# Three quarters of an MLP's first product as seven products of blocks, with tokens halved

## The chip, the cores and the metric

The kernel runs on one core of one Trainium2 chip. The metric is the device time of one execution in microseconds. One run is profiled as well; its rows and its trace are read below. PE is TensorE's matmul row, PEld its weight loads, DVE is VectorE, ACT is ScalarE, POOL is GpSimd and SP issues most of the transfers.

## The reference

A two-layer encoder with 512 tokens of 1024 features, batch 1, all in float32. Layer 0 mixes with stick-breaking attention, layer 1 with a gated linear recurrence; each is followed by the MLP, which is what changes here.

```
for layer in range(2):
    h = rms_norm(x, norm_mix[layer])
    x = x + (stick_breaking_attention(h, ...) if layer == 0 else rglru_block(h, ...))
    h = rms_norm(x, norm_mlp[layer])
    u = relu(h @ mlp_w1[layer])            # 512 x 1024 @ 1024 x 4096
    x = x + (u * u) @ mlp_w2[layer]        # 512 x 4096 @ 4096 x 1024
return rms_norm(x, norm_final)
```

## The kernel before

Activations lie with features on the 128 partitions and tokens along the free dimension: `x[c]` is a chunk of 128 features by 512 tokens, c = 0..7. A float32 product is made of three float32r matmuls: each operand is split into a high half (a cast, on ACT) and a low half (operand minus high half, on DVE), and high x high, low x high and high x low are summed in a bank. For the MLP's input the halves are `xgh` and `xgl`. For a slab of weights `raw`, 128 x 1024, they are `wh` and `wl`; the DVE instruction that makes `wl` is called a cut below. Four pairs of buffers `wh`/`wl` exist.

The MLP goes through the 4096 hidden features in four quarters of 1024 (`Mlp.quarters`).

*First product* (`squared`): for each of eight chunks of 128 hidden features, a slab of `w_m1` is loaded, cut, and multiplied with all tokens: 8 steps of k by 3 matmuls of 512 columns, so 192 matmuls a quarter (lines 209 to 211). ACT applies relu and square into `u`.

*Second product* (`down`): tokens, hidden features and outputs are halved, and the 2 x 2 blocks are multiplied by the seven products P1 to P7 (a scheme of Winograd's kind). `u` holds per unit of 256 hidden features the four blocks, from which DVE makes four sums in place (`sums`); `split` makes their high halves (`bh`, `sh`) on ACT and their low halves (`bl`, `sl`) on DVE. Blocks of weights `b11`, `b12`, `b22`, 128 x 2 x 512, are loaded ahead (`load`), `b21` on use. P5, P6, P7 and P4 need sums of blocks, made in place on DVE (line 865); only in the last quarter P7's and P4's (layer 0) or P4's (layer 1) are made by an accumulating transfer from POOL's queue. Each product is made for two halves g of the quarter ("P5 1" is P5 for the second half): 2 token slices x 2 x 3 matmuls of 512 columns, 12 a product, 168 a quarter (line 877). `collect` adds a finished bank, scaled per token, into `c`.

The order of PE is as written; the other engines' queues are put in order by the compiler's scheduler and are then fixed. Two dense chunks of the next quarter's first product are put ahead of each second product but the last:

```
                for c in range(2):
                    self.squared(q4 + 1, c)
                self.down(q4)
                self.sums(0)
                self.split(0)
```

In layer 1 the residual `x` is transposed and added to the output in the last quarter (`between`); in layer 0 the output is transposed back and added to `x` after it (`feature`). `x` stays in SBUF meanwhile.

Of the kernel before, what the change touches and what calls it, by code (L numbers as in the profile page):

```python
# [48 lines left out]
def hybrid_encoder(  # L49
# [10 lines left out]
    w_m1: bass.AP,  # L60
    w_dn: bass.AP,
# [666 lines left out]
    class Mlp:  # L728
# [10 lines left out]

        PRODUCTS = {  # L740
            "P1": (0, "b11", None, "X", 0, False),
            "P5": (4, "b11", "b12", "V", 3, False),
            "P6": (5, "b11", "b22", "X", 1, True),
            "P3": (6, "b22", None, "V", 1, False),
            "P7": (1, "b12", "b22", "X", 3, True),
            "P2": (2, "b21", None, "W", 0, False),
            "P4": (3, "b11", "b21", "X", 2, False),
# [5 lines left out]
        def __init__(self, ctx, layer):  # L753
            self.layer, self.sq, self.first = layer, Squares(), None
            self.mp = ctx.enter_context(tc.tile_pool(name=f"mlp{layer}", bufs=2))
            self.c = [
                self.mp.tile([P, 2, S], F32, tag=f"c{i}", name=f"c{i}", bufs=1) for i in range(4)
            ]
            self.begun, self.a = set(), {}
            self.turns = count()  # L760
            self.blocks = ExitStack()
            self.bp = self.blocks.enter_context(tc.tile_pool(name=f"blocks{layer}", bufs=2))
            self.u, self.raws = {}, {}
# [9 lines left out]
        def squared(self, q4, c, ready=None):  # L773

            if self.first is None:
                self.first = [self.bank() for _ in range(2)]
                ws = [slab(w_m1[self.layer, i]) for i in range(2)]
                beside(ws, xgh, xgl, self.first, {})
            if self.first:
                ps = self.first.pop(0)  # L780
            else:
                ps = dense(
                    w_m1[self.layer, q4 * C + c], xgh, xgl, halves=ready, ps=self.bank()
                )
            j, a = divmod(c, 2)
            if a == 0:
                self.u[j] = self.mp.tile([P, BLOCKS, HS], F32, tag="u", name="u", bufs=1)
            t = self.u[j][:, 2 * a : 2 * a + 2, :].rearrange("p i n -> p (i n)")
            A.activation(t, ps, AF.Relu)
            A.activation(t, t, AF.Square)  # L790
            if q4 == 0:

                if c in range(2, C - 2):
                    for i in range(2):
                        self.sq.chunk(2 * (c - 2) + i, x[2 * (c - 2) + i])
                if c == C - 1:
                    self.rr = self.sq.inv_squares(self.bank())
            return t

        def sums(self, j):  # L800

            u = self.u[j]
            for out, x, y, op in (
                (4, 1, 3, ALU.subtract), (5, 4, 0, ALU.subtract), (6, 5, 2, ALU.add),
                (1, 0, 1, ALU.subtract),
            ):
                V.tensor_tensor(u[:, out, :], u[:, x, :], u[:, y, :], op)  # L807

        def split(self, j):
            if j < 2:  # L810
                n = BLOCKS * HS
                h, l = (
                    t.rearrange("p c s -> p (c s)")[:, j * n : (j + 1) * n].rearrange(
                        "p (i n) -> p i n", n=HS
                    )
                    for t in (bh, bl)
                )
            else:
                h, l = (
                    self.bp.tile([P, BLOCKS, HS], F32R, tag=t, name=t) for t in ("sh", "sl")  # L820
                )
            u = self.u[j]
            A.copy(h, u)  # L823
            self.ready = V.tensor_tensor(l, u, f(h), ALU.subtract)  # L824
            self.a[j] = h, l

        def weights(self, q4, g, tag):
            return w_dn[self.layer, q4, g, *self.SOURCES[tag]]

        def load(self, q4):  # L830

            for g in range(2):
                for tag in ("b11", "b12", "b22"):
                    t = self.bp.tile([P, 2, S], F32, tag=tag, name=tag)
                    nc.sync.dma_start(out=t, in_=self.weights(q4, g, tag))
                    self.raws[tag, g] = t
# [10 lines left out]
        def block(self, q4, name, g, far):  # L847

            _, b, to, *_ = self.PRODUCTS[name]
            if b == "b21":  # L850
                t = wpool.tile([P, C, P], F32, tag="raw", name="raw", bufs=3)
                t = t.rearrange("p (j k) f -> p j (k f)", j=2)
                nc.sync.dma_start(out=t, in_=self.weights(q4, g, b))
                self.raws[b, g] = t
            raw = self.raws[b, g]
            if name in far:

                G.dma_start(out=raw, in_=self.weights(q4, g, to), accum_op=ALU.add)  # L858
            elif to:

                ahead = None
                if far and (name, g) != ("P5", 0):
                    ahead = self.ready if name == "P5" else self.before
                with tc.issue_after(ahead.ins) if ahead else nullcontext():
                    self.sum = V.tensor_tensor(raw, raw, self.raws[to, g], ALU.add)  # L865
            return self.operand(raw)

        def times(self, name, g, i, w, ps, new, cols=slice(0, S)):
# [4 lines left out]
            for jj in range(2):  # L873
                h, l = self.a[2 * g + jj]
                first, last = new and g == jj == 0, g == jj == 1
                for n, (x, y) in enumerate(((h, wh), (h, wl), (l, wh))):
                    PE.matmul(  # L877
                        ps, x[:, block, ts], y[:, jj, cols], start=first and n == 0,
                        stop=last and n == 2, skip_group_check=not new,
                    )  # L880
# [12 lines left out]
        def down(self, q4, far=(), end=None):  # L893
            sums, last_cut = {}, {}

            def product(name, g, w=None):
                w = w or self.block(q4, name, g, far)
# [13 lines left out]
            if end is None:  # L911
                for name in ("P1", "P5", "P6", "P3", "P7", "P2", "P4"):
                    for g in range(2):
                        product(name, g)
                return

            order = [("P1", 0), ("P5", 0), ("P2", 0), ("P1", 1), ("P2", 1), ("P5", 1)]
            order += [(name, g) for name in ("P6", "P3", "P7", "P4") for g in range(2)]
            ws = {}

            def prepare(*at):

                if at != ("P7", 1):
                    self.before = self.cut
                ws[at] = self.block(q4, *at, far)
                last_cut[at[0]] = self.cut
# [8 lines left out]

        def quarters(self, between, far, end):
            loaded = {}
            for q4 in range(NQ):
                last = q4 == NQ - 1
                for c in range(2 * (q4 > 0), C):  # L940

                    with tc.high_priority() if last and c > C - 3 else nullcontext():
                        self.squared(q4, c, loaded.pop(c, None))
                        if c % 2:
                            self.sums(c // 2)
                            self.split(c // 2)
                    if last and c == C - 3:
                        loaded = {i: slab(w_m1[self.layer, q4 * C + i]) for i in (C - 2, C - 1)}
                    if c == 3 - 3 * (q4 == 0):
                        self.load(q4)  # L950
                    between(q4, c)
                if last:
                    self.down(q4, far, end)
                    break

                for c in range(2):
                    self.squared(q4 + 1, c)
                self.down(q4)
                self.sums(0)
                self.split(0)  # L960
            self.blocks.close()

    with ExitStack() as mctx:
        mlp = Mlp(mctx, 0)
        squares = Squares()
# [23 lines left out]
        def between(q4, c):  # L989
            if (q4, c) == (0, C - 1):  # L990
                soft.send(mlp.ready)

        mlp.quarters(between, ("P7", "P4"), end)
# [186 lines left out]
    with ExitStack() as mctx:  # L1180
# [3 lines left out]
        def between(q4, c):  # L1184

            t = c - 2
            if q4 < NQ - 1 or t not in range(NB):
                return
            for h in range(2):
# [5 lines left out]
                V.tensor_tensor(mlp.y(t, h), mlp.y(t, h), pt, ALU.add)  # L1195

        gb = lp.tile([P, D], F32, tag="gb", name="gb")
        nc.sync.dma_start(out=gb, in_=g_final.broadcast_to([P, D]))
# [16 lines left out]
        def scaled(t, h, cols=slice(0, S)):  # L1215
            y = mlp.y(t, h)[:, cols]
            G.tensor_tensor(y, y, gb[:, h * S : (h + 1) * S][:, cols], ALU.mult)

        def finish(t, h, i, cut=None, last=None):
# [8 lines left out]
            with tc.issue_after(last.ins) if last else nullcontext():  # L1228
                V.scalar_tensor_tensor(
                    y[:, cut:], y[:, cut:], rt, gb[:, h * S : (h + 1) * S][:, cut:],  # L1230
# [31 lines left out]

        mlp.quarters(between, ("P4",), end)
# [65 lines left out]
```

## Time and profile before

| | us |
|---|---|
| median of 3 runs | 1076.51 |
| lowest and highest | 1075.07, 1077.06 |
| the profiled execution | 1076.9 |
| its span | 1075.1 |

In the span PE is busy 1059.4 us, DVE 782.4, ACT 599.6 and POOL 166.8. Layer 0's MLP lies at about 250 to 583 us of the span, layer 1's from about 734 on. A row of grouped instructions reads: line, engine, operation, tiles, shapes, count, busy time and mean ns of one, idle time ahead of them and who ended it. A row of the timeline reads: start in us, duration, engine, line, tiles, and in brackets the idle time before it.

### The profile page before, as it was taken

Reading aid. Unit: us, or ns where it says so; the run is one execution under the profiler, and the core shown is the slowest. Engines: PE = TensorE matmul, PEld = TensorE weight load, DVE = VectorE, ACT = ScalarE, POOL = GpSimd, SP = SyncE. Lnnn points to the kernel's source line nnn. Section 1 sums busy time; section 2 is a strip of 40 time slices with the busy share of each in tenths; the row PEclk is TensorE's granted clock in tenths of the full one; section 3 lists DMA queues with packets and bytes.
Section 4 is the critical chain, followed back from the end, with each engine's and each line's share of the span. In section 5 each row is a group of like instructions: output and inputs, shape, how many; then the busy total and the mean of one; then the engine's idle time right before and its main releaser. Section 6 shows DMA issues by size and latency. Waiting matters only on the chain.

```text
span 1075.1 us, 13570 instructions
## 1 busy us (share of the span) xinstructions
PE 1059.4 (99%) x5004; PEld 879.4 (82%) x5004; DVE 782.4 (73%) x1020; ACT 599.6 (56%) x888; POOL 166.8 (16%) x192
## 2 busy tenths in 40 slices
PE   9999999999999999999999999999999999999997
PEld 7888888888888888888878777888888888888875
DVE  7788787838686596597578878974676597497667
ACT  6777676826554543544546477944554544544346
POOL 2344443510000000000001655000000000000005
PEclk9999999999999999999999999999999999999999
DMA  7745454517215206206341785252215206305104
GB/s 236 198 117 148 122 147 108 170 52 249 85 49 187 79 31 187 96 20 191 84 98 60 180 211 129 87 191 82 79 43 190 82 22 189 103 20 176 59 6 112
DMA packets 44033, 125.70 MB, mean 117 GB/s; under 512 B 7744, under 2 KB 8512, under 8 KB 43968
## 3 DMA queue, kind: packets, MB, share of 16 engines
q1 hardware_dynamic: 41088, 115.94, 34.8%
q0 software_dynamic: 2304, 8.39, 4.5%
q8 instruction: 39, 0.64, 0.2%
q10 hardware_dynamic: 576, 0.52, 0.1%
q14 instruction: 26, 0.21, 0.1%
HBM read 104.91 MB, written 2.10 MB: 100 GB/s over the span
## 4 chain that ended last, share of the span: by engine, by line
PE 86%; DVE 5%; ACT 3%; issue 2%; POOL 2%; DMA 1%; SPq 0%; ACTq 0%; DVEq 0%; POOLq 0%
PE ps_t L877 8%; PE ps_acc L877 7%; PE ps_o L877 6%; PE ps_acc L211 6%; PE ps_acc L209 6%; PE ps_acc L210 6%; PE ps_z L877 5%; PE ps_t L209 4%; PE ps_t L210 4%; PE ps_t L211 4%; PE ps_o L209 4%; PE ps_o L211 4%; PE ps_o L210 4%; PE ps_z L210 3%; PE ps_z L211 3%; PE ps_z L209 3%
## 5 line engine op out<-in xcount | busy, mean ns | idle before, releaser
L204 DVE TENSOR_TENSOR wl<-raw,wh 128x1024 fp32r<-128x1024 f32 (+2 forms) x126 | 130.5, 1052 | 89.7 <-ACT wh L197 89.5
L843 ACT CAST wh<-b 128x1024 fp32r<-128x1024 f32 x96 | 100.0, 1048 | 122.2 <-PE ps_t L877 23.3
L197 ACT CAST wh<-raw 128x1024 fp32r<-128x1024 f32 (+2 forms) x136 | 119.5, 898 | 66.9 <-PE ps_acc L877 10.2
L844 DVE TENSOR_TENSOR wl<-b,wh 128x1024 fp32r<-128x1024 f32 x96 | 116.5, 1221 | 41.6 <-ACT wh L843 40.9
L209 PE MATMUL ps_acc<-xgh,wh 128*128 128x512 f32 x288 | 116.0, 403 | 1.0 <-ACT wh L178 0.9
L210 PE MATMUL ps_acc<-xgh,wl 128*128 128x512 f32 x288 | 112.7, 391 | 0.3 <-DVE wl L179 0.3
L211 PE MATMUL ps_acc<-xgl,wh 128*128 128x512 f32 x288 | 112.6, 391 | 0.1
L858 POOL DMA_DIRECT2D b<-in_w_dn x6 | 5.4, 904 | 680.9 <-DVE wl L844 358.7
L209 PE MATMUL ps_t<-xgh,wh 128*128 128x512 f32 x200 | 78.7, 394 | 0.0
L210 PE MATMUL ps_t<-xgh,wl 128*128 128x512 f32 x200 | 78.0, 390 | 0.0
L211 PE MATMUL ps_t<-xgl,wh 128*128 128x512 f32 x200 | 77.8, 389 | 0.0
L561 DVE TENSOR_TENSOR_SCAN scan<-keep,later 128x128 f32<-128x128 f32 (+1 forms) x64 | 58.4, 916 | 17.6 <-ACT keep L551 10.8
L211 PEld LDWEIGHTS ps_acc<-xgl,wh 128*128 128x128 f32 x288 | 54.1, 188 | 12.0 <-DVE xgl L118 0.5
L209 PE MATMUL ps_o<-xgh,wh 128*128 128x512 f32 x160 | 63.1, 394 | 0.2 <-DVE x L713 0.2
L209 PEld LDWEIGHTS ps_acc<-xgh,wh 128*128 128x128 f32 x288 | 54.2, 188 | 10.9 <-ACT wh L178 1.1
L211 PE MATMUL ps_o<-xgl,wh 128*128 128x512 f32 x160 | 62.3, 390 | 0.0
L210 PE MATMUL ps_o<-xgh,wl 128*128 128x512 f32 x160 | 62.3, 389 | 0.0
L210 PEld LDWEIGHTS ps_acc<-xgh,wl 128*128 128x128 f32 x288 | 54.3, 188 | 9.6 <-DVE wl L179 1.0
L565 POOL TENSOR_TENSOR w<-w,scan 128x128 f32<-128x128 f32 (+1 forms) x64 | 53.5, 838 | 52.5 <-DVE scan L561 49.5
L865 DVE TENSOR_TENSOR b<-b,b 128x1024 f32<-128x1024 f32 x46 | 56.1, 1222 | 0.9
L807 DVE TENSOR_TENSOR u<-u 128x256 f32<-128x256 f32 x128 | 49.5, 419 | 0.7
L824 DVE TENSOR_TENSOR bl<-u,bh 128x1792 fp32r<-128x1792 f32 x16 | 32.4, 2025 | 22.9 <-ACT bh L823 22.9
(332 smaller groups left out, 2761.6 us busy)
## 6 DMA issues: line engine op xcount, KB each, us to landing
raw<-in_w_m SPq DMA_DIRECT2D x64, 512.0 KB, 3.5
b<-in_w_dn SPq DMA_DIRECT2D x48, 512.0 KB, 3.6
raw<-in_w_dn SPq DMA_DIRECT2D x16, 512.0 KB, 3.5
raw<-in_w_in SPq DMA_DIRECT2D x16, 512.0 KB, 4.0
raw<-in_w_qk SPq DMA_DIRECT2D x12, 512.0 KB, 3.5
wl<-raw POOLq DMA_DIRECT2D x10, 512.0 KB, 6.2
x<-in_xT SPq DMA_DIRECT2D x16, 256.0 KB, 4.2
raw<-in_w_ro SPq DMA_DIRECT2D x8, 512.0 KB, 4.3
```

What stands on the lines that cost most here:

```text
L197: A.copy(wh[:, k, :], raw[:, k, :])
L204: V.tensor_tensor(wl[:, k, :], raw[:, k, :], f(wh[:, k, :]), ALU.subtract)
L209: PE.matmul(ps, wh, ah, start=start, stop=False)
L210: PE.matmul(ps, wl, ah, start=False, stop=False)
L211: PE.matmul(ps, wh, al, start=False, stop=stop)
L561: V.tensor_tensor_scan(sc[:, S - n : S][:, ::-1], keep[:, :n][:, ::-1], later[:, S - n :][:, ::-1], 1.0, ALU.mult, ALU.max,)
L565: G.tensor_tensor(wt, wt, sc[:, S - n + 1 : S + 1], ALU.mult)
L807: V.tensor_tensor(u[:, out, :], u[:, x, :], u[:, y, :], op)
L843: A.copy(wh, raw)
L844: self.cut = V.tensor_tensor(wl, raw, f(wh), ALU.subtract)
L865: self.sum = V.tensor_tensor(raw, raw, self.raws[to, g], ALU.add)
L877: PE.matmul(ps, x[:, block, ts], y[:, jj, cols], start=first and n == 0, stop=last and n == 2, skip_group_check=not new,)
```

## The change

The first quarter's first product stays dense. The first products of quarters 1 to 3 are now also made by seven products (`up`): features, hidden features and tokens are halved, in two units p of 512 hidden features. Weights are the stationary operand, tokens the moving one, with 256 columns instead of 512: a unit has 7 products x 2 x 4 x 3 matmuls. P1, P5 and P6 share banks with later products and are first copied out (`kept`) by ACT; DVE combines them with P3, P7 and P2; relu and square follow, then the sums and splits for the second product. The blocks of a unit's u are kept in one buffer `u` with one copy, taken in turn by the two units.

- The sums of x that the seven products need are made once, in the first quarter: `sums_of_x` scales x by its gains in place and sums blocks on DVE, `halves_of_sums` makes the halves. They lie in x's own place, so x is stored to DRAM (`away`) in the first quarter and in layer 0 loaded again before the last second product (`back`). `replace` puts halves over parts of `xgh` when the dense product is done.
- In layer 1 x is transposed into the output at the start (first quarter) rather than added in the last.
- Of the four sums of weights of each set of products, P7's and P4's are made by accumulating transfers, in the first and the second product; in the last quarter's second product it is as before.
- The order of the second product's steps is given by `ORDERS`: "first" for the first quarter, "mid" for the second and third, "last" for the last. In "mid" it is P1 0, P5 0, P1 1, P2 0, P5 1, P6 0, ...; in "first" P2 0 stands ahead of P1 1; in "last" P2 1 comes before P5 1 too.
- The two dense chunks ahead of a second product are gone; it follows P4 of the second unit.
- The final gains `gb` are loaded later, and the table for the square root is loaded early in layer 1.

```
@@ quarters
+            for q4 in range(NQ):
+                if q4:
+                    del self.u[0], self.u[1], self.a[1]
+                    for p in range(2):
+                        self.up(q4, p, units[p], self.FAR_UP)
+                        units[p] = self.from_down(q4, p)
+                last = q4 == NQ - 1
+                if last:
+                    end.ready()
+                    self.down(q4, units, far, end)
+                    break
+                self.down(q4, units, self.FAR_DOWN)
+                if q4 == 0:
+                    self.replace()
+                units = [self.from_up(q4 + 1, p) for p in range(2)]
...
+        def up(self, q4, p, unit, far):
+            u = self.u_tile(p)
+            banks, kept = {}, {}
+            for name in ("P1", "P5", "P6", "P3", "P7", "P2", "P4"):
+                w = [t.rearrange("p j n -> p (j n)") for t in self.block(unit, name, far)]
+                w = [t.rearrange("p (k n) -> p k n", n=2 * P) for t in w]
+                block, _, _, to, *_ = self.PRODUCTS[name]
+                new = to not in banks
+                if new:
+                    banks[to] = self.bank()
+                ps = banks[to]
+                for i in range(2):
+                    for k in range(C // 2):
+                        h, l = self.xa(block, k)
+                        wh, wl = (t[:, k, i * P : (i + 1) * P] for t in w)
+                        for n, (m, y) in enumerate(((wh, h), (wl, h), (wh, l))):
+                            PE.matmul(ps[:, i * HS : (i + 1) * HS], m, y, ...)
+                three = ps.rearrange("p (i n) -> p i n", i=2)
+                if name in ("P1", "P5", "P6"):
+                    t = work.tile([P, S], F32, tag="sq" if name == "P1" else "r", name="kept")
+                    A.copy(t, ps)
+                    kept[name] = t.rearrange("p (i n) -> p i n", i=2)
+                    continue
...
+                if name == "P3":
+                    V.tensor_tensor(t, three, kept[one], op)
+                elif one:
+                    V.tensor_tensor(t, kept[one], three, op)
+                A.activation(t, t if one else three, AF.Relu)
+                self.square(t)
+                if name == "P2":
+                    self.split(p, slice(0, 2), slice(0, 3), slice(0, 3))
+            self.sums(p, slice(0, 2))
+            for i in range(2):
+                self.split(p, i, slice(0, 4), slice(3, 7))
...
+        def sums_of_x(self, k):
+            lo, hi = slice(0, HS), slice(HS, S)
+            u, v = x[k], x[C // 2 + k]
+            for c in (k, C // 2 + k):
+                g = col(f"mlp{self.layer}")[:, c : c + 1]
+                A.activation(x[c], x[c], AF.Identity, scale=g)
+            V.tensor_tensor(v[:, hi], u[:, hi], v[:, hi], ALU.subtract)
+            V.tensor_tensor(u[:, hi], u[:, lo], u[:, hi], ALU.subtract)
+            V.tensor_tensor(u[:, lo], v[:, hi], u[:, lo], ALU.subtract)
+            V.tensor_tensor(v[:, lo], u[:, lo], v[:, lo], ALU.add)
...
+        def replace(self):
+            for i, t in enumerate(self.s3):
+                A.copy(xgh[:, 2 * i : 2 * i + 2, HS:], f(t).rearrange("p (k n) -> p k n", k=2))
...
+        FAR_UP, FAR_DOWN = ('P7', 'P4'), ('P7', 'P4')
...
-            if name in far:
-                G.dma_start(out=raw, in_=self.weights(q4, g, to), accum_op=ALU.add)
+            if to and name in far:
+                G.dma_start(
+                    out=raw.rearrange("p j n -> p (j n)"), in_=unit["src"](to), accum_op=ALU.add
+                )
```

291 lines of the change are left out of this document (186 added, 105 removed), and 3 rows, old and new, of the table ORDERS.

## The prediction

> **What bounds the kernel now.** I read the page first, then who waits for whom on PE, then the stretches of the MLPs stage by stage.
>
> ```profile
> span 1075.1 us, 13570 instructions
> PE 1059.4 (99%) x5004; PEld 879.4 (82%) x5004; DVE 782.4 (73%) x1020; ACT 599.6 (56%) x888; POOL 166.8 (16%) x192
> ```
> ```profile
> PE ps_o L1105 <- ACT bh L1091: 2.2, 1, 2.2
> ...
> PE ps_t L877 <- DVE wl L844: 1.0, 2, 0.6
> PE ps_t L877 <- DVE c L888: 0.9, 2, 0.5
> ```
> ```profile
> core 0: us, PE busy (x) PEld busy (x) DVE busy (x) ACT busy (x) POOL busy (x), PEclk, DMA share, GB/s
> 343.10:386.40 43.30, 43.30 (x192) 35.86 (x192) 26.71 (x29) 20.18 (x24) 0.00 (x0) 1.00 0.23 74
> 386.40:424.60 38.20, 38.20 (x169) 31.47 (x169) 30.34 (x34) 18.21 (x19) 0.00 (x0) 1.00 0.44 138
> 539.10:583.00 43.90, 42.75 (x193) 34.06 (x193) 36.10 (x42) 21.10 (x25) 5.12 (x5) 1.00 0.36 83
> ```
>
> PE is busy 99% of the span and loses some 2 us to others in all the MLPs (the two L877 rows). The second view gives a quarter: the first product of one quarter (dense, 192 matmuls of 512 columns) takes 43.3 us, the second product (already seven products) 38.2 us, neither with idle time on PE. DVE is at 62% in the dense stretch and 79% in the other. So every matmul saved shortens the span, as long as DVE and ACT keep ahead of PE. The last quarter's stretch (539 to 583) is the one where PE already lost 1.2 us.
>
> **What the matmuls save.** Matmuls overlap, so I price them by the distance of starts.
>
> ```profile
> 304.59 1.36 PE ps_t L877 x6
> ```
> ```profile
> 142.99 0.28 PE L458 MATMUL ps_acc<-wh,xgh 128*128 128x256 f32 x1
> ...
> 144.42 0.40 PE L209 MATMUL ps_acc<-xgh,wh 128*128 128x512 f32 x1
> ```
>
> Six matmuls of 512 columns take 1.36 us, 0.227 each. Twelve of 256 columns (L458 to L460) start between 142.99 and 144.42: 0.119 each, not half of 0.227. A new quarter has 2 units x 7 products x 2 x 4 x 3 = 336 matmuls of 256 columns, 336 x 0.119 = 40.0 us, against 192 x 0.227 = 43.6. The gain is 3.6 us a quarter and, with three quarters in two layers, 22 us.
>
> [...] The trace has 227 and 119 ns, and its numbers decide.
>
> **What DVE and ACT must do in exchange.** Prices, with the starts of consecutive instructions behind them:
>
> ```profile
> L844 DVE TENSOR_TENSOR wl<-b,wh 128x1024 fp32r<-128x1024 f32 x96 | 116.5, 1221 | 41.6 <-ACT wh L843 40.9
> L807 DVE TENSOR_TENSOR u<-u 128x256 f32<-128x256 f32 x128 | 49.5, 419 | 0.7
> L824 DVE TENSOR_TENSOR bl<-u,bh 128x1792 fp32r<-128x1792 f32 x16 | 32.4, 2025 | 22.9 <-ACT bh L823 22.9
> L713 DVE TENSOR_TENSOR x<-x,ps_o 128x512 f32<-128x512 f32 x8 | 5.4, 683 | 8.0 <-PE ps_o L211 8.0
> L843 ACT CAST wh<-b 128x1024 fp32r<-128x1024 f32 x96 | 100.0, 1048 | 122.2 <-PE ps_t L877 23.3 <-DVE b L865 20.4 <-PE ps_acc L877 17.1
> L823 ACT CAST bh<-u 128x1792 fp32r<-128x1792 f32 x16 | 27.1, 1692 | 22.7 <-DVE u L807 18.1 <-PE ps_t L877 1.5 <-PE ps_acc L877 1.5
> L789 ACT ACTIVATE u<-ps_o 128x512 f32<-128x512 f32 x18 | 10.7, 597 | 32.9 <-PE ps_o L211 20.1 <-issue 8.5 <-DVE bl L824 2.3
> L790 ACT ACTIVATE u<-u 128x512 f32<-128x512 f32 x64 | 39.5, 633 | 0.5
> ```
> ```profile
> 391.51 1.22 DVE L844 TENSOR_TENSOR wl<-b,wh 128x1024 fp32r<-128x1024 f32 x1
> 392.65 0.75 DVE L807 TENSOR_TENSOR u<-u 128x256 f32<-128x256 f32 x2
> 393.32 0.74 DVE L888 SCALAR_TENSOR_TENSOR c<-ps_t,rr,c 128x512 f32<-128x512 f32 x1
> 393.98 1.21 DVE L865 TENSOR_TENSOR b<-b,raw 128x1024 f32<-128x1024 f32 x1
> 395.11 2.35 DVE L844 TENSOR_TENSOR wl<-b,wh 128x1024 fp32r<-128x1024 f32 x2
> ```
>
> A cut (wl) or sum of weights of 1024 blocks DVE for 1.14 us (391.51 to 392.65, 393.98 to 395.11), a collect for 0.66; instructions overlap by about 0.08. By that the 1792-wide split is 1.94 and a 1536-wide one 1.68, a 512-wide sum 0.60 (0.66 where each needs the one before). One new unit costs DVE 7 cuts and 2 sums (10.2), 3 combinations out of the banks (1.8), a split of 1536, 4 sums of u (2.6) and 2 splits of 1024: 18.5 us, 37 a quarter against 40.0 of PE. Before it was 27. ACT: 7 casts, 3 copies of banks, 4 relus and squares and 3 casts of u, about 16 us a unit. Both fit on average. The second product loses four sums of weights (to accumulating transfers), 4.5 us of DVE, which PE does not see. So the inside of a quarter I cost at 0: I followed it in the order of the built program, and each operand's halves are done 1.5 us or more before PE wants them.
>
> What does not fit is the passage from first to second product. In the kernel before, two dense chunks of the next quarter (10.9 us) stand between the last split and P1, and a unit's split is spread over a quarter. Now the second unit's P4 ends 0 us before P1 0. Only four pairs wh/wl exist, so a cut can't start before PE has finished the product four places back.
>
> ```profile
> 402.62 0.39 PE L877 MATMUL ps_t<-wh,bh 128*128 128x512 f32 x1
> 402.82 1.05 ACT L843 CAST wh<-b 128x1024 fp32r<-128x1024 f32 x1 [1.70 <-PE ps_t L877]
> 403.90 1.23 DVE L844 TENSOR_TENSOR wl<-b,wh 128x1024 fp32r<-128x1024 f32 x1 [0.21 <-ACT wh L843]
> 403.98 0.39 PE L877 MATMUL ps_acc<-wh,bh 128*128 128x512 f32 x1
> ...
> 406.62 1.23 DVE L844 TENSOR_TENSOR wl<-raw,wh 128x1024 fp32r<-128x1024 f32 x1 [1.49 <-ACT wh L843]
> 407.76 0.75 DVE L888 SCALAR_TENSOR_TENSOR c<-ps_t,rr,c 128x512 f32<-128x512 f32 x1
> ```
>
> PE frees a pair at 402.62, the cast starts 0.2 later, and the cut 1.08 after that. DVE keeps its order: bank t was finished at 403.98, but its collect waited behind a cut that waited 1.49 us. [...]
>
> *Second and third quarter (order "mid").* From the end of P3 in the second unit, when the pair for P1 0 comes free, to the last wait of P5 1 on a split, PE has 3 x 2.86 + 4 x 2.73 (12 x 0.227) + 1.1 = 20.6 us of work. In that time the built program's DVE queue holds: 6 cuts, 4 sums of weights, 4 splits of 1024 (14 x 1.14 = 15.9), the split of 1536 (1.7), 3 combinations (1.8), 4 sums of u (2.6), 2 collects (1.3): 23.3. It begins 1.25 late (0.2 and a cast) and waits 0.35 for the relu, square and cast of P2's block. 24.9 - 20.6: PE stands 4.3 us in P5 1. Four such quarters: 17.
>
> *Last quarter.* P5 1 comes one product later, PE's cover is 3 x 2.86 + 5 x 2.73 + 0.2 = 22.4. DVE has 12 x 1.14 + 1.7 + 1.8 + 2.6 + 1.3 = 21.1, begins 1.25 late and waits 3.9 for ACT (P2's chain, the last casts), since P5 1's sum stands behind the splits: 26.2, 3.8 short, and the next two products, P6 0 and P6 1, whose sums and cuts follow on the same queue, lack 1.5 more. 5.3 in each layer, less the 1 us that PE loses there already.
>
> *First quarter.* Its product stays dense, and DVE gets 16 sums of x and 12 low halves (11 us) more. In ACT's queue the two copies that replace halves of xgh stand ahead of the last casts of u, and they wait for the last dense matmul. After it DVE first waits 3.1 us (0.2, those copies, two squares, a cast). In layer 0 its queue up to the last split then holds 5 cuts, 2 sums of weights, 2 splits of 768 and 2 of 1024 and 8 sums of 256 columns (0.35 each): 15 us, so 18.1, where P5 1 wants that split after four products and 1.1 us, at 12.0: 6 us. In layer 1 a collect of P1 1 stands in DVE's queue ahead of P5 1's cut, and DVE comes to it 0.5 us after P1 1 has ended; from there to the last split stand 4 cuts, a sum of weights, 2 collects, 2 short sums and the split, 8.9 us and waits for two casts of 0.8: 10.2 against 1.1, 9 us.
>
> Bounds: without any wait for ACT the four mid passages cost 2.7 each, the last ones 0, the first ones what the queue alone gives behind the end of P1 1, 2.5 and 7.5: 21 in all. At the other end ACT and the transfers come later than I take: 2 us more at each of six places, 55. I take 6 + 9 + 17 + 10.6 = 43.
>
> **Other parts.** An accumulating transfer landed in 5.4 us, a plain one in 3.6:
>
> ```profile
> b<-in_w_dn SPq DMA_DIRECT2D x48, 512.0 KB, 3.6
> b<-in_w_dn POOLq DMA_DIRECT2D x6, 512.0 KB, 5.4
> ```
>
> P7's is released by P5's sum and P4's by P6's cut, three or more products ahead (8 us): 0, and if late, it is DVE's cut that waits, behind which the combinations queue. POOL has nothing else there. x goes to DRAM and back in 16 transfers of 256 KB on SP; the loads stand ahead of one block's load (P1 1's b11) in the last quarter, which still has some 5 us. PE's 32 transposes in layer 1 only move from the last quarter to the first.
>
> **Sum.** The profiled execution took 1076.9 us (span 1075.1), 0.4 above the median of the three runs, 1076.5. 1076.5 - 22 + 43 - 1 = 1096.5; I say 1096 us.
>
> **Rivals.** *A, the passages are covered* (faster): the transfers' relief and the prefetch of four pairs let DVE be past the splits when P5 1 comes. For it: the average load is 37 of 40 us, and the kernel before ran DVE at 79% in the second product without a wait. It decides where the stalls sum to under 20 us, so below half of mine; with 0 to 20 it gives 1054 to 1074, in the middle 1064. Against it: four pairs bound the prefetch. Chance 0.15. *B, stalls at the low bound*, 20 to 30 us: 1074 to 1084; it holds "no change" and a little slower. Chance 0.15. *C, weight loads set the pace:*
>
> ```profile
> L458 PEld LDWEIGHTS ps_acc<-wh,xgh 128*128 128x128 f32 x112 | 21.2, 189 | 0.6
> ```
>
> In runs of 256 columns PEld has next to no idle time. There two of three matmuls share the stationary operand; in the new product it changes each time. If a load of 0.189 then can't overlap its neighbour, a quarter takes 336 x 0.189 = 63.5 us, 20 more than before, and the passages are covered better: 1076.5 + 6 x 20 = 1196. [...] Against it: the 119 ns include one change in three and show no slower third. Chance 0.03. That the sevenfold product isn't done is excluded: the built program has 864 matmuls more.
>
> **How the numbers follow.** Forecast (stalls of 30 to 55 us, 1084 to 1110): 0.67. A measurement of this kernel tells 0.2%, 2 us. Faster: A, 0.15, and a little of B: 0.16. Same, 1074.4 to 1078.6: 0.05 out of B. Slower: 0.79. The range 1075 to 1110 leaves out A, nearly, and C.
>
> **What would show it.** In the profile after, starts of 256-column matmuls in the new product lie 0.119 apart; PE waits for DVE "sl" and "wl" at P5 1, once in each quarter, longest in layer 1's first (right: 4 to 9 us each, 40 in sum; wrong: under 20). If PE waits inside the new product, on wl or on a bank, the price of the inside is wrong; if DVE has idle time in the passage ahead of the splits, ACT or a transfer is what is late.

## The result, and the profile after

The changed kernel takes 1100.73 us, median of four runs (1099.62 to 1102.88), against 1076.72 beside it: a ratio of 1.0229, 95% interval 1.0210 to 1.0247. It is 24 us slower; I had said 1096. The profiled execution took 1100.7 us, its span is 23.9 us longer than that of before.

The page, the waits of PE and the stretches of the two MLPs (first products and second products in turn, each from its first matmul to the next stage's) after the change:

```profile
span 1099.0 us, 15815 instructions
PE 1053.4 (96%) x5868; PEld 912.1 (83%) x5868; DVE 867.1 (79%) x1120; ACT 676.4 (62%) x1025; POOL 205.1 (19%) x240
```
```profile
PE ps_t L913 <- ACT u L934: 10.8, 4, 2.7
PE ps_t L1004 <- ACT sh L825: 8.2, 2, 5.8
PE ps_z L913 <- DVE u L933: 2.7, 1, 2.7
PE ps_z L913 <- ACT u L934: 2.7, 1, 2.7
```
```profile
core 0: us, PE busy (x), PEclk, DMA share, GB/s
293.38:336.68 43.30, 40.44 (x169) 0.96 0.52 125
336.68:379.07 42.39, 39.69 (x338) 1.00 0.64 158
379.07:419.10 40.03, 38.88 (x170) 1.00 0.58 146
419.10:463.06 43.96, 41.26 (x338) 0.96 0.65 156
463.06:502.03 38.97, 38.79 (x170) 1.00 0.60 151
502.03:545.90 43.87, 41.17 (x337) 0.96 0.77 203
545.90:589.65 43.75, 41.30 (x186) 1.00 0.36 77
790.13:838.98 48.85, 42.26 (x170) 0.90 0.51 123
838.98:883.26 44.28, 41.60 (x337) 0.96 0.60 150
883.26:922.55 39.29, 39.12 (x170) 1.00 0.59 149
922.55:967.66 45.11, 42.42 (x337) 0.93 0.62 151
967.66:1007.13 39.47, 39.44 (x169) 0.99 0.60 151
1007.13:1051.43 44.30, 41.62 (x337) 0.96 0.54 139
1051.43:1091.95 40.52, 39.47 (x181) 1.00 0.23 52
```

The same stretches of the kernel before (first, middle and last second product of layer 0 with a dense first product between, then first and last of layer 1):

```profile
304.43:342.70 38.27, 38.27 (x170) 1.00 0.42 137
342.70:386.22 43.52, 43.52 (x194) 1.00 0.23 74
538.91:580.87 41.96, 40.98 (x185) 1.00 0.38 88
788.58:827.26 38.68, 38.68 (x169) 1.00 0.42 136
1027.92:1068.40 40.48, 39.51 (x180) 1.00 0.24 52
```

The balance, against what I forecast:

| part | forecast, us | measured, us |
|---|---|---|
| six new first products (263.9 against 6 x 43.52) | -22 | +2.8 |
| second products of quarters 2 and 3 | +17 | +3.9 |
| second products of quarter 4 | +10.6 - 1 | +1.8 |
| second products of quarter 1 (43.30, 48.85) | +15 | +15.2 |
| sum | +20 | +23.7 |

The sum is near; the parts are not. The new first product takes 42.4 to 45.1 us, 44.0 on average, where the dense one takes 43.5, and in quarters 2 to 4 the passage behind it costs little.

**Where PE waits.** Each of the six new products stands still for 2.7 us once (the rows with L913: 16.2 us), always at the second unit's last product, P4. In the first of them (DVE, then PE):

```profile
370.00 1.22 DVE L826 TENSOR_TENSOR bl<-u,bh 128x1024 fp32r<-128x1024 f32 x1
371.14 1.22 DVE L991 TENSOR_TENSOR b<-b,b 128x1024 f32<-128x1024 f32 x1
372.27 1.22 DVE L826 TENSOR_TENSOR bl<-u,bh 128x1024 fp32r<-128x1024 f32 x1
373.55 1.23 DVE L972 TENSOR_TENSOR wl<-b,wh 128x1024 fp32r<-128x1024 f32 x1
374.69 0.68 DVE L931 TENSOR_TENSOR u<-ps_t,kept 128x512 f32<-128x512 f32 x1
375.29 0.68 DVE L933 TENSOR_TENSOR u<-kept,ps_t 128x512 f32<-128x512 f32 x1
376.12 0.36 PE L913 MATMUL ps_t<-xgh,wh 128*128 128x256 f32 x1 [2.70 <-ACT u L934]
```

P4 adds to bank X, on top of P7, and DVE must have read P7 out of it first (L933; the instruction that does it is called P7's combination). That combination stands in DVE's queue behind the first unit's splits (L826) and behind the sum and cut of the second product's P5 0 (L991, L972). The releaser named is a relu (L934), but the start at 376.12 follows the end of L933, 375.97. PE's operands for P4 had long been there.

**What follows a wait.** Behind the wait of the second new product, matmuls of 256 columns go out 0.21 us apart instead of 0.12 for some 3 us; behind the long waits of the first quarters those of 512 columns go out 0.43 us apart instead of 0.227. The granted clock is 0.50 there. The first two rows hold the wait of the first new product (373.42 to 376.12), which no such stretch follows; the other two hold that of the second (456.05 to 458.75) and what follows it:

```profile
371.17:374.59 3.42, 2.25 (x19) 1.00 0.25 19
374.59:378.00 3.41, 1.88 (x16) 1.00 0.74 139
456.51:459.92 3.41, 1.17 (x10) 1.00 0.86 139
459.92:463.33 3.41, 3.41 (x18) 0.50 0.10 22
```

By the clock's own record in this trace, its falls in the MLPs begin at 309.73, 459.92, 541.84, 804.67, 879.76, 961.68 and 1047.01 us. Between them lie 44, 24, 77, 22, 24 and 25 times 3.413 us; five last 3.41 us, that at 804.67 lasts 10.24 and that at 961.68 6.83. In the 3.41 us ahead of each of the seven TensorE is idle for 1.67 to 2.70 us. The first new product's wait falls into two stretches that lie 18 and 19 times 3.413 us behind the first fall (the first two rows), with 1.2 and 1.5 us of idle time; the second's lies mostly in one, with 2.2.

The first new product takes 42.39 - 2.86 = 39.5 us without its wait (2.86 us more than the pitch from start to start). The other five, less their waits, take 41.0 to 42.3, so 1.5 to 2.7 us more each, for the most part at half clock. Over both MLPs the starts of some 120 matmuls are so spread, about 14 us in all, against about 1 before.

### The profile page after: what moved, and what is told of

The parts are those of the page before. It is cut to its first block, busy times and chain, and to the rows that moved or that the text cites. A ratio compares the mean times of both kernels' runs of the same rounds, so it can differ in the third digit from the quotient of the medians.

```text
span 1099.0 us, 15815 instructions
## 1 busy us (share of the span) xinstructions
PE 1053.4 (96%) x5868; PEld 912.1 (83%) x5868; DVE 867.1 (79%) x1120; ACT 676.4 (62%) x1025; POOL 205.1 (19%) x240
## 4 chain that ended last, share of the span: by engine, by line
PE 73%; DVE 13%; ACT 6%; issue 4%; DMA 2%; POOL 1%; SPq 0%; ACTq 0%; DVEq 0%; POOLq 0%
PE ps_t L913 7%; PE ps_z L913 7%; PE ps_acc L1004 6%; PE ps_t L1004 6%; PE ps_o L1004 5%; PE ps_z L1004 4%; PE ps_acc L212 4%; PE ps_acc L210 4%; PE ps_acc L211 4%; PE ps_o L913 3%; DVE wl L972 2%; ACT wh L971 2%; PE ps_o L210 2%; DVE b L991 2%; PE ps_o L212 2%
## 5 line engine op out<-in xcount | busy, mean ns | idle before, releaser
L971 ACT CAST wh<-b 128x1024 fp32r<-128x1024 f32 x168 | 174.3, 1049 | 186.6 <-DVE b L991 74.3
L972 DVE TENSOR_TENSOR wl<-b,wh 128x1024 fp32r<-128x1024 f32 x168 | 204.3, 1223 | 75.6 <-ACT wh L971 74.4
L198 ACT CAST wh<-raw 128x512 fp32r<-128x512 f32 (+2 forms) x88 | 69.5, 819 | 37.2 <-DMA raw<-in_w_in 10.4
L205 DVE TENSOR_TENSOR wl<-raw,wh 128x512 fp32r<-128x512 f32 (+2 forms) x78 | 71.1, 938 | 16.5 <-ACT wh L198 16.3
L991 DVE TENSOR_TENSOR b<-b,b 128x1024 f32<-128x1024 f32 x58 | 70.3, 1220 | 0.3
L913 PE MATMUL ps_t<-xgh,wh 128*128 128x256 f32 x144 | 43.1, 299 | 10.8 <-ACT u L934 10.8
L972 DVE TENSOR_TENSOR wl<-raw,wh 128x1024 fp32r<-128x1024 f32 x28 | 34.2, 1223 | 18.9 <-ACT wh L971 18.8
L913 PE MATMUL ps_z<-xgh,wh 128*128 128x256 f32 x144 | 42.5, 295 | 5.4 <-DVE u L933 2.7
L835 DVE TENSOR_TENSOR u<-u 128x512 f32<-128x512 f32 (+1 forms) x80 | 46.5, 582 | 1.3
L913 PE MATMUL ps_t<-low,wh 128*128 128x256 f32 x160 | 44.8, 280 | 0.0
L826 DVE TENSOR_TENSOR sl<-u,sh 128x1024 fp32r<-128x1024 f32 (+2 forms) x26 | 33.4, 1304 | 12.1 <-ACT sh L825 12.1
```

Of the source, the lines that this page charges most:

```text
L198: A.copy(wh[:, k, :], raw[:, k, :])
L205: V.tensor_tensor(wl[:, k, :], raw[:, k, :], f(wh[:, k, :]), ALU.subtract)
L913: PE.matmul(ps[:, i * HS : (i + 1) * HS], m, y, start=new and i == k == n == 0, stop=i == 1 and k == C // 2 - 1 and n == 2, skip_group_che ...
L971: A.copy(wh, raw)
L972: self.cut = V.tensor_tensor(wl, raw, f(wh), ALU.subtract)
L991: self.sum = V.tensor_tensor(raw, raw, unit[to], ALU.add)
```

## Experiments

Two theories. *Load*: from the end of P3 to the last split VectorE has more to do than TensorE has cover; the order decides only where TensorE stands. *Order* (later called *queue*): TensorE stands because what it needs is queued behind something that itself waits or isn't needed yet.

**e1, the order alone.** In quarters 2 to 4 the combinations go ahead of P5 0's sum and cut:

```diff
+ with tc.issue_after(self.combined.ins):       # P7's combination, second unit
      w = self.block(units[0], "P5", far)
+ # cuts from P6 1 on: behind the last splits
```

> Only the order of VectorE's queue is changed: in quarters 2 to 4 the second unit's combinations of P3 and P7 stand ahead of the sum and the cut of P5 0 (before: behind them), and the later cuts stay behind the splits. Nothing is added or left out. Theory 'load' (VectorE has 23 us of work between the end of P3 and the last split that P5 1 needs, TensorE 20.6 us to cover it; where TensorE stands is only a matter of the order): the wait of 2.85 us ahead of P4 falls to 0.3-0.5, and the waits at P5 1 grow by the same 2.4, to 2.5-4 us each; time 1095-1101. Theory 'order' (TensorE stands ahead of P4 only because its bank is read behind P5 0's cut): P4's wait falls to 0.3-0.5 and P5 1's stay at 0.3-1.5; six times 2.4 and the slow matmuls behind them go: 1080-1086.

1115.93 us, ratio 1.0362 (1.0330 to 1.0393): 15 us slower than the change. First and second product of quarter 2, layer 0, and the two waits of this passage:

```profile
337.08:377.23 40.15, 39.69 (x338) 1.00 0.59 155
377.23:423.06 45.83, 41.65 (x171) 0.93 0.58 140
```
```profile
384.30 0.50 PE L1010 MATMUL ps_acc<-wh,sl 128*128 128x512 f32 x1 [0.97 <-DVE sl L827]
392.75 0.79 PE L1010 MATMUL ps_z<-wh,sh 128*128 128x512 f32 x1 [3.17 <-ACT sh L826]
```

The wait at P4 is down to 0.6 us, the new product to 40.15 us, and the stall stands at P5 1, where I had forecast it, 3.2 us with 1 us more at P1 1. In the last quarters too 0.6 us are left at P4, and P5 1 waits 5.6, for a cast behind a late sum. "Order" is refuted: nothing is won by moving the stall. "Load" has the direction, its size was too small: the passage takes 45.8 instead of 40.0 us, since VectorE is idle 0.9 and 1.1 us in the scheduler's new order and slow matmuls follow the longer wait. It also prices the matmuls alone: 40.15 less 0.6 is 39.5 us against my 40.0.

**e2, less work for VectorE.** P5's and P6's sums by adding transfers too, in quarters 1 to 3:

```diff
- FAR_UP, FAR_DOWN = ('P7', 'P4'), ('P7', 'P4')
+ FAR_UP, FAR_DOWN = ('P7', 'P4'), ('P5', 'P6', 'P7', 'P4')
```

> In quarters 1 to 3 of the second product, P5's and P6's sums of weights are made by adding transfers too, so VectorE is relieved of four sums, 4.6 us, in each of these passages; the scheduler orders the queues anew and puts the combinations of P3 and P7 ahead of P5 0's cut, but the last splits behind the cuts of P6 1 and P3 0, the last of which waits for a pair that P2 0 frees. Theory 'load': 4.6 us less is more than the 3.2 to 4.4 that TensorE stands in each passage of quarters 2 and 3, so both waits go there, and the first quarters lose 2 us less each: 1072-1080. Theory 'order' (what stands ahead in the queue decides, not its length): P4's wait goes, but P5 1 waits 3 us for the splits behind P3 0's cut in each of these quarters: 1092-1099. If the transfers come too late (5.5 us each, 20 of 24 more in all), TensorE waits at P5 0 or P6 1 for a cut.

1148.13 us, ratio 1.0647 (1.0627 to 1.0668). Both theories missed it, by 49 us and more. The last sentence named the late transfers, but neither the size nor the place: in the first passage ACT stands at three casts that wait for them (4.2, 2.9 and 6.1 us), the splits come behind, and PE waits for those, 2.8 us at P1 1 and 5.3 at P5 1, and hardly for a cut.

**e3, both**, with all cuts for the products behind P5 1 behind the last splits.

```diff
+ behind = [self.combined] if q4 and (name, g) == ("P5", 0) else []
+ if order.index((name, g)) > order.index(("P5", 1)):
+     behind += [self.ready, self.cast]         # last split: VectorE, ScalarE
```

> The two together: P5's and P6's sums by adding transfers in quarters 1 to 3, the combinations ahead of P5 0's sum and cut in all of quarters 2 to 4, and in quarters 1 to 3 all work for the products behind P5 1 stands behind the last splits. 'Load': VectorE's queue in the passage of quarters 2 and 3 is 18.7 us and 1.6 of waits, against 20.6 of cover: waits at P4 and P5 1 under 0.5 us each; the first quarters lose 1 us (layer 0) and 2 us (layer 1) instead of 5 and 10; the last ones keep 1-2 us at P5 1 and P6: 1065-1073. 'Order' gives the same here. If the transfers set the pace: TensorE waits for a cut of P5 or P6, 1-3 us a quarter, 1075-1090.

1134.78 us, ratio 1.0538 (1.0514 to 1.0562). ACT in the first passage, and the transfer of P5 0 that it waits for:

```profile
373.99 0.86 POOL L988 DMA_DIRECT2D b<-in_w_dn  x1 [0.48 <-DVE wl L974]
381.14 2.00 ACT L973 CAST wh<-b 128x1024 fp32r<-128x1024 f32 x2 [3.76 <-DMA b<-in_w_dn]
383.04 0.62 ACT L936 ACTIVATE u<-u 128x512 f32<-128x512 f32 x1
```

The transfer starts when P1 0 has been cut (373.99) and the cast of its result starts 7.2 us later. Behind that cast, in ACT's queue, stands the relu of the second unit's block (383.04), 6 us after its operand; the splits follow it, and PE waits for them at P1 1 (2.8 and 0.6 us). So, by these rows, a sum on a transfer relieves VectorE only where 7.2 us lie between the cut before it and the cast behind it; P5, one or two products behind P1, has no such room. Queue against load is not decided by e2 and e3.

**e5, the first quarter**: e3, and the last halves of sums of x and the copies into xgh behind the last split.

```diff
+ with tc.issue_after(ready.ins), tc.issue_after(cast.ins):
+     for k in (2, 3): self.halves_of_sums(k)
      self.replace()
```

> As the third kernel of this job, and in the first quarter the halves of the sums of x for the last two pairs of chunks and the two copies that replace halves of xgh stand behind the last split on VectorE and ScalarE. If these 3.1 us of VectorE and 4.4 us of ScalarE ahead of the splits are what makes the first quarters late: their waits at P5 1 go from 1 and 2 us to under 0.5, 2-4 us less than the third kernel. If not (the casts of u, or P1 1's collect ahead of P5 1's cut, set it): within 1 us of it. They must then be done before the new product begins, some 30 us later; no wait is expected there.

1130.50 us, ratio 1.0506 (1.0478 to 1.0534). Its median is 4 us below e3's, though the times of the two overlap (1129.98 to 1136.62 against 1133.01 to 1139.08). The gain that the rows show is in layer 1's first quarter, whose second product takes 41.4 instead of 44.3 us; in layer 0 it is 46.2 in both, where P5 1 waits for its transfer.

**e6, more cover**: the last quarter's order of products (P2 1 ahead of P5 1) in quarters 2 and 3 too, with e1's combinations ahead of P5 0's sum and cut. e1's other half is left out: here the cuts from P6 1 on are not held behind the last splits.

```diff
- order = self.ORDERS["last" if end else "mid" if q4 else "first"].split()
+ order = self.ORDERS["last" if q4 else "first"].split()
```

> Quarters 2 and 3 take the second product's order of the last quarter (P2 1 comes ahead of P5 1, which gives TensorE 2.7 us more of work before P5 1 and VectorE 1.1 us more), with the combinations ahead of P5 0's sum and cut as in the first kernel run; everything else on VectorE is where the scheduler puts it, and it puts the last sums of u and the last splits behind P6 1's and P3 0's cuts and P2 1's collects, which wait for P1 1 and P2 1 to end. 'Load' (the sum of work against the cover): the cover grows by 1.6 us net, P5 1's 4 us become 2-2.5 in these four quarters; 1104-1109 against 1115.9 of the first kernel run. 'Queue' (what stands ahead of the split and waits for TensorE decides): P5 1 waits 3.5-5 us, no gain: 1113-1121.

1130.72 us, a single time. The wait at P5 1 in the first passage:

```profile
396.05 0.80 PE L1006 MATMUL ps_z<-wh,sh 128*128 128x512 f32 x1 [6.30 <-ACT sh L825]
```

The cover grew by 2.7 us and the wait at P5 1 from e1's 3.2 to 6.3: the scheduler used VectorE, busy nearly all through, for later products' cuts and collects. From P7's combination to the last splits there are eight cuts and four collects, in e1 five and two. Here the queue decides, as that theory said, and more than it said. What the longer cover alone is worth, with e1's other half kept, was not run.

**f2, f3, f4, the queue written by hand.** VectorE's passage of quarters 2 to 4 becomes a chain in which each instruction is issued after the one before, in an order in which none waits long for TensorE; the order of products is that of e6, and P6's sums are adding transfers (not P6 1's in the first quarter). f3 adds the first quarter's change of e5; f4 is f3 with P6's sums on VectorE.

```diff
+ def before(n):
+     if n == 0:
+         block("P1", 0); pair = self.pair()
+         # each behind the one before: sum P5 0, cut P2 0, cut P5 0,
+         # split of blocks 0 to 2, cut P1 1, four sums of u
+     elif n == 1:   # sum P5 1, cut P2 1
+     elif n == 2:   # cut P5 1, last splits; then P1 1's collects
```

> In quarters 2 to 4 VectorE's queue from the combinations to the last split is written out by hand, so that nothing in it waits for TensorE: combinations, P5 0's sum, the cuts of P2 0 and P5 0, the first split, P1 1's cut, four sums of u, P5 1's sum, the cuts of P2 1 and P5 1, the last splits, then collects. P2 1 comes ahead of P5 1, P6's sums are made by adding transfers (but P6 1's in the first quarter). By that queue the splits end 2 us before P5 1 wants them. 'Queue': P4 waits 0.6 us, P5 1 and P6 0.0-0.5, the new first products take 40.2-40.8 us and the second products of quarters 2 and 3 38.3-39.5; only the first quarters still lose 4-8 us each: 1066-1078. 'Load' (it can't fit): waits of 1-3 us at P6 and P3 in each of these quarters, and slow matmuls behind them: 1085-1100.

> As the kernel before it, and in the first quarter the halves of the sums of x for the last two pairs of chunks and the two copies that replace halves of xgh stand behind the last split. If these are what makes the first quarters late, their waits at P5 1 go to 0-1.5 us, and it is 3-7 us faster than the kernel before it: 1060-1072. If P1 1's collect and the casts of u set it, within 1.5 us of it.

> As the kernel before it, but P6's sums are made by VectorE, as in the changed kernel; they stand behind the last splits. 'Queue': P6 0's cut comes 1 us later and is still in time, P6 1's is 0.5 us late: 0-4 us slower than the kernel before it. 'Load' (two sums, 2.3 us, are too much): waits of 1-2.5 us at P6 in each of six quarters with slow matmuls behind them, 10-20 us slower.

f2 1085.04 us, 1.0072 (1.0049 to 1.0096); f3 1083.46, 1.0075 (1.0056 to 1.0094); f4 1100.19, 1.0219 (1.0204 to 1.0235). f2 lies above what "queue" had said and at the lower edge of "load". f3's first-quarter change is worth 1.7 us in layer 1 and nothing in layer 0, and the medians of f2 and f3 don't tell it from noise. f4 against f3 is the price of twelve sums, 13.7 us of VectorE: 16.7 us of time, as "load" had said (10 to 20). But 7.7 us of it lie in the two first quarters, where only one sum each, 1.14 us, goes back to VectorE: where a sum stands counts beside its length. f4, whose VectorE has the changed kernel's sums, takes the changed kernel's time, 1100.2 against 1100.7, with its waits at P6 0 (2.6 us in the first passage) instead of P4; its first quarters are 4.7 us shorter, the rest as much longer. So three orders with this work (the changed kernel's, e1's, f4's) put the stall at three products, and none is without it; that no order would be is argued, not shown. Taking work away helps, where the transfers have room. In f3 part of what is left is queue:

```profile
409.59 1.05 ACT L976 CAST wh<-b 128x1024 fp32r<-128x1024 f32 x1 [5.00 <-DMA b<-in_w_up]
410.67 1.22 DVE L977 TENSOR_TENSOR wl<-b,wh 128x1024 fp32r<-128x1024 f32 x1 [2.29 <-ACT wh L976]
411.81 0.74 DVE L1020 SCALAR_TENSOR_TENSOR c<-ps_z,rr,c 128x512 f32<-128x512 f32 x1
412.61 0.50 PE L1009 MATMUL ps_z<-wh,bh 128*128 128x512 f32 x1 [2.29 <-DVE c L1020]
```

The cut for the next quarter's P1 waits for a load, P7's collect stands behind it, and PE waits for the bank.

**f5 and f6, two more passes over the queue.** f5: P5 1's cut ahead of the sums of u, P7's collects ahead of the next quarter's first cut, P6's transfers in layer 1's last quarter too. f6: cuts of P4 and of the second unit's P1 behind P7's combination in the new product.

```diff
+ behind = {"P1": self.read if p else self.seven, "P4": self.read}.get(name)
+ with tc.issue_after(behind.ins) if behind else nullcontext():
+     w = self.block(unit, name, far)
```

> As the kernel with the written queue and the first quarter's change, with three more places in it: P5 1's cut stands ahead of the four sums of u (so that the adding transfer of P6 1, which it releases and which took 6.6 us to land, starts 3 us earlier; in the last run TensorE waited 1.7 us for it, at P6 1), P1 1's collects ahead of the last splits and P2 1's behind P6 1's cut; P7 1's collects ahead of the first cut of the next quarter's product (that cut waited for a load, and TensorE waited 1.1 to 2.5 us for the bank behind it, at P4); layer 1's last quarter takes transfers for P6 too. 'Queue' (each wait left is an operand or a bank behind a queued instruction that itself waits): those waits fall to 0.0-0.5 and the second products of quarters 2 and 3 take 38.4-39.5 us (before: 38.3 and 38.7): 1062-1070, faster than before the change. 'Load' (VectorE or the transfers are simply full): the waits move to another product of the same quarters, and it stays within 4 us of 1083.5.

> As the last kernel, with one more place in VectorE's queue: inside the new first product the cut of P4 (both units) and the second unit's P1 cut stand behind P7's combination instead of ahead of it. In the last run P4's cut waited for its transfer (issued 419.7, landed about 427.5), the combinations stood behind it, and TensorE waited for the bank at the first unit's P4 in five of six quarters: 2.7, 1.8, 0.4, 0.9 and 1.0 us, with slow matmuls behind the longest. 'Queue': these waits fall to 0.0-0.6, the new first products take 40.2-41.0 us in all six quarters: 1064-1070, ratio to before 0.988-0.994. 'Load': the same waits come back as waits for P4's or P1's operands: 1072-1076.

f5 takes 1074.49 us, ratio 0.9972 (0.9955 to 0.9989): 26 us faster than the change, and a little faster than the kernel before. It lies between what the two theories said (1062 to 1070, and 1079.5 to 1087.5). VectorE's work is that of f3 (854 us against 853), so most of these 9 us against f3 are the queue's. Its stretches in layer 0, from the second quarter's first product on:

```profile
334.99:375.14 40.15, 39.68 (x337) 1.00 0.61 156
375.14:413.85 38.71, 38.71 (x171) 1.00 0.80 190
413.85:456.93 43.08, 40.09 (x338) 1.00 0.59 147
456.93:495.79 38.86, 38.69 (x171) 1.00 0.79 190
```

These second products are within 0.6 us of those before. The first unit's P4 now waits up to 2.7 us (the third quarter's product, 43.08). f6 was to end that, and took 1096.48 us, 1.0195 (1.0171 to 1.0220): the waits at the first unit's P4 are gone, but I had put the second unit's P4 cut behind that unit's combinations as well, and PE waits 1.4 and 0.7 us there for a half and again at the next splits, in all six quarters.

**f7**: f6 without that mistake.

```diff
- behind = {"P1": self.read if p else self.seven, "P4": self.read}.get(name)
+ behind = {"P1": self.read if p else self.seven, "P4": None if p else self.read}.get(name)
```

> As the kernel with the second queue (1074.5 us), with the first unit's P4 cut and the second unit's P1 cut behind the first unit's P7 combination, and the second unit's P4 cut left where it was: the run before had it behind that unit's combination too, which come as late as 370.8 (behind the first unit's splits), so that TensorE waited 1.3-1.7 and 0.9 us for P4's halves and 0.6-1.1 and 0.8 us for the splits behind it in each of six quarters. 'Queue': the waits at both P4s are under 0.6 us, new first products 40.2-41.0 us, second products as in the second queue (38.7-39.4): 1064-1070, ratio 0.987-0.994. 'Load': within 2 us of 1074.5.

1082.02 us, 1.0047 (1.0029 to 1.0066): slower than f5, and not as expected by either theory.

```profile
333.50:377.42 43.92, 41.47 (x337) 0.96 0.59 146
377.42:415.71 38.29, 38.29 (x170) 1.00 0.74 190
```
```profile
365.06 2.00 ACT L981 CAST wh<-b 128x1024 fp32r<-128x1024 f32 x2 [2.29 <-DMA b<-in_w_up]
366.14 1.23 DVE L982 TENSOR_TENSOR wl<-b,wh 128x1024 fp32r<-128x1024 f32 x1 [1.83 <-ACT wh L981]
```

The second product is at the time of before to 0.02 us, and each new first product again loses 2.4 to 2.8 us at the second unit's P4. The place is that of the changed kernel, but the cause in the rows is the adding transfer of that P4: its cast waits for it, and the sum of u, the first unit's splits and the combinations come behind. The rows say why it is late: in f5 that transfer is issued 22.0 us into the first new product (356.98), in f7 26.0 us (359.51), since here two of the first unit's combinations stand ahead of the second unit's cuts and wait 2.8 and 2.1 us for PE. This is read from the two traces, not tried.

**e8, one part undone**: the changed kernel without adding transfers.

```diff
- FAR_UP, FAR_DOWN = ('P7', 'P4'), ('P7', 'P4')
+ FAR_UP, FAR_DOWN = (), ()
```

> The changed kernel with one part undone: no adding transfers, so P7's and P4's sums of weights (in all quarters of both products) are VectorE's, 4 more a quarter in each product, 1.14 us each; all else, the order of the products too, is the changed kernel's. 'Load': three more of these sums lie between the end of P3 and the last split, 3.4 us, which TensorE stands longer in each of six passages, and the first quarters 1-3 us: 1118-1130. 'Queue': the scheduler now puts P1 1's cut ahead of the combinations, which waits for the pair that P2 frees, so P4 waits 3.5-5 us instead of 2.85, and P5 1 2-4 us instead of 0.3-1.5: 1115-1130 too; the two differ in the place: by 'load' alone P4's wait is 2.9 + 1.1 (the one sum that stands ahead of it).

1138.02 us, 1.0566 (1.0546 to 1.0585): 37 us slower than the change, for 925.2 us of VectorE instead of 867.1; both theories had said 15 to 30.

```profile
342.60:390.36 47.76, 42.25 (x338) 0.93 0.29 89
390.36:430.42 40.06, 38.75 (x170) 1.00 0.32 105
```

P4 waits 5.5 us in quarters 2 and 3. One more cut and one more sum stand ahead of the combinations there; "queue" had named the cut, and both theories said less (3.5 to 5 us, and 4.0). P5 1 waits 1.3 us, not the 2 to 4 of "queue", and the second product is as in the changed kernel. The transfers were worth having; by themselves they were not enough.

## Why the prediction's number came out right, point by point

- *The matmuls, 3.6 us a quarter.* Right: 39.5 us without waits (e1, the changed kernel's first) against 40.0 forecast. Rival C, weight loads at 0.189, is refuted: the load changes with each matmul and the pitch stays at 0.12.
- *"So the inside of a quarter I cost at 0".* Wrong, and the step that failed. I had followed the operands' halves and not the bank: P4's accumulation waits for P7's combination, which I counted among DVE's work but in no place. 17 us of waits from start to start and 9.6 more, most of it slow matmuls behind them. This ate the gain: +2.8 instead of -22. The prediction had named such a wait, on a bank inside the new product, as a sign that its price of the inside is wrong.
- *Quarters 2 and 3, 4.3 us each at P5 1.* The queue was right (23.3 us of work on 20.6 of cover), the place wrong. In the first passage PE waits 2.86 at P4 and 1.16 and 0.33 at P5 1, 4.35 in all; in the other three 3.2. Since PE had already stood at P4, P5 1 found its splits nearly ready. With the wait at P4 gone (e1) it appears at P5 1. Over all quarters P5 1 waits 13 us from start to start; 40 were forecast, and under 20 was to count as wrong.
- *Last quarters, 5.3 us each.* 2.86 us are lost at the first product's P4 and none at P5 1. The second product's two P6 lose 1.4 together, as the forecast had it (1.5); its P6 and P4 lost 1.3 before the change.
- *First quarters, 6 and 9 us.* The waits are 3.2 and 7.3. The slow matmuls behind them make it 5.0 and 10.2, so that 15.2 against 15 is luck. In layer 0 I had VectorE's first split wait until 3.1 us behind the last dense matmul, for the copies into xgh. They ran before its end (290.15 and 291.72), and the split began at 293.11, just ahead of P1 0 (293.38). In layer 1 VectorE came to P1 1's collect at 799.89, 1.2 us before P1 1's end and not 0.5 behind it.
- *No term for slow matmuls.* I used one pitch throughout. The trace of before had the evidence: behind its one wait of 2.2 us (L1105, quoted for another purpose) six matmuls go out 0.43 us apart. About 13 us.
- *Adding transfers at 0.* Right for P7 and P4 in the changed kernel (e8 shows what they save). Not so as a rule: e3 shows what one costs where the next cast is less than 7.2 us away.
- *Rival A.* A passage that is covered does exist (f5, f7: second products of 38.3 to 39.4 us), with the queue written out and P6's sums away; neither half was enough alone (f4 has the queue without the relief, e2 and e3 have P5's and P6's relief without the queue by hand; P6's alone, in the scheduler's queue, was not run). Even so the range that I gave A, up to 1074, was not quite reached, since a wait comes back in the first product. B is out: the waits alone are 32 us more than before.

So the mechanism, VectorE's work between two products delaying TensorE, was right in kind; its main place was wrong, and the total came out near by luck: the slow matmuls that I left out (13 us) stand for what I counted too much in waits (42 against 32). What stays open: whether a queue exists that has neither f5's wait nor f7's, and how much of the loss an order alone could win back with the changed kernel's sums.

## What to carry to other kernels

Follow each accumulating matmul's bank as well as its operands: who reads it last, and what stands ahead of that reader in its queue. Where an engine has more work in a passage than the next one has cover, moving instructions may only move the stall, as in e1 and f4, and removing work shortens it (f3 against f4); then look at what each waiting instruction holds up behind it (f5 against f3). A sum moved to a transfer is free only if the cast that needs it isn't at the head of a queue before it lands (7.2 us from its start to that cast in e3).

## What the runs showed of the hardware

A wait of TensorE cost more than itself: with waits of 2.3 to 5.8 us the granted clock fell to half (0.50 in the rows above), for 3.4 us, once 6.8 and once 10.2, in seven of the eight such waits in the MLPs of the changed kernel. The length of a wait alone does not tell: the changed kernel's of 2.33 us (to 307.46) has a fall behind it, its first of 2.70 (to 376.12) has none, nor has f5's of 2.52 (to 433.57; clock 1.00 from 413.85 to 456.93). In f6 two waits within about 1 us of each other, of 1.35 and 0.69 us (to 372.62), left it at 1.00 in the first passage (333.17 to 416.59). Over the whole profiled run the clock was 0.983 on average in the changed kernel, 0.988 in f6, 0.996 in f5 and 0.997 before.

An adding transfer of 512 KB, 5.4 us in the kernel before, lay 7.2 us before the cast that waited for it in e3.
